# GpSimd's large-tile elementwise work moves to VectorE, and the experts' weights are split in halves of 1024 columns

## The chip, the cores and the metric

The kernel runs on one core of one Trainium2 chip. The metric is the device time of one execution in microseconds (us); the time before is the median of three runs, 1736.25 us. TensorE multiplies matrices, VectorE (DVE in the rows), ScalarE (ACT) and GpSimd (POOL) do elementwise work, each with its own queue that is worked off in order; SyncE (SP) issues the loads of the weights.

## The reference, cut to what matters

Two layers over 256 latent and 256 context tokens with 1024 features each, all in float32. Layer 0 has a gated short convolution and a dense SwiGLU network, layer 1 a differential attention and eight SwiGLU experts, of which each latent token takes two. Each norm is followed by a modulation from a conditioning vector:

```python
def modulate(xn, shift, scale):
    return xn * (1 + scale) + shift

def swiglu(a, w1, w3, w2):
    return (jax.nn.silu(a @ w1) * (a @ w3)) @ w2

for i in range(DEPTH):
    sh1, sc1, g1, sh2, sc2, g2 = adaln(c, ada_w[i], ada_b[i])
    a = modulate(rms_norm(h, norm_mix_g[i]), sh1, sc1)
    ...
    h = h + g1 * y
    a = modulate(rms_norm(h, norm_ffn_g[i]), sh2, sc2)
    ...
```

The hidden width is 2816 in every SwiGLU (22 feature tiles of 128), so the experts are eight times 11 chunks of two feature tiles.

## The kernel before

A float32 product is made of three matmuls on numbers of twelve bits: each operand is the exact sum of a high part and a low part, and `mm3` (L178 to L180) multiplies high by high, low by high and high by low. The weights come from memory in units of 1 MB, 128 partitions by 2048 columns. `Loads` issues their loads on SP in the order of use, whenever a slot for a raw unit (names `rw`, `ra`, `rp`, `rq`, `xl`, `xt`) comes free. `Parts.pump` then makes the two parts: ScalarE casts the raw unit into the high part `wh` (L79), and the low part `wl` is the raw unit minus the high part, a TENSOR_TENSOR of L83 with two inputs in SBUF. Three slots hold such pairs of parts (four in the experts), so a unit is split two or three units ahead of the matmuls that use it, as soon as TensorE is done with an older unit.

Which engine takes L83 is told by `engines(u)`, by the number u of the unit. Units 0 to 48 are layer 0, 49 to 64 the attention's first ones, from 69 on come the experts, three units to a chunk:

```python
if u >= 69:
    return [(slice(0, 1024), [(V, slice(0, 768)), (PO, slice(768, 1024))]), (slice(1024, U), [(V, slice(1024, 1664)), (PO, slice(1664, U))])]
pool = u < 12 or 12 < u < 49 and u % 2 or u == 59 or u > 60
```

Here V is VectorE and PO is GpSimd. GpSimd takes more than that: the modulation of every second or so feature tile in three operations (L322, L323, L315; VectorE needs two, L325 and L317, with ScalarE's cast L326 between), the adds of half of the context's first squares (`more`), four small products of the rotary step (L705) for each tile of queries or keys, and one scaling of heads (L697).

The stages in their order: the start (0 to 86 us in the trace), where the modulation's vectors are made by long sums over the conditioning matrices on VectorE (`ada`, L258, `junk`: one operation of 1024 columns with two SBUF inputs, accumulated into a column, four to a unit) and the first six feature tiles of the convolution's input product follow the modulated tiles as they come; the convolution (to 228 us), with eight groups of five VectorE operations `conv(j)` (L490 to L499) and 12 units of `ada` between them; the dense network (to about 635 us); the attention; the routing; and the experts (from 889 us). In a chunk of an expert, TensorE makes two tiles of the hidden layer `h` with 24 matmuls of 512 columns, transposes the gated tile `ga` (L1143), and adds 12 matmuls into `y`; the order on VectorE is `ga` (L1137), splits, `hl` (L1147, the low part of the hidden tile, which the last third of `y` waits for), splits. During chunks 2 to 9 of odd experts, and at some others, gathers for the next experts are put between (`g`, L1098 on TensorE; L1092 and L1102 on VectorE). All orders are written by hand; no scheduler changes them.

Of the kernel before, what the change touches and what calls it, by code (L numbers as in the profile page):

```python
# [37 lines left out]
class Loads:  # L38
    """Units of weights, [128, 2048] each, loaded in their order as slots come free."""
# [23 lines left out]
class Parts:  # L63
    """The units as exact sums of two parts of twelve bits, made ahead of their use."""
# [24 lines left out]
    def unit(self):  # L89
        """The next unit, for use until the next call that takes one, or until release() if it is held."""  # L90
        if not self.holding:
            self.release()
        if self.cur not in self.got:
            self.pump()
        self.spent.append(self.cur)
        self.cur += 1
        return self.got[self.cur - 1]

    def __next__(self):
        """The next block of 128 columns."""  # L100
# [8 lines left out]
    def release(self, most=99):  # L109
        """Gives back what is used up."""  # L110
# [7 lines left out]
    def give(self, n):  # L118
        """Gives back the first n of the units that are held."""
# [10 lines left out]
def backbone(ctx: ExitStack, tc: tile.TileContext, i, out, stage=9):  # L130
# [16 lines left out]
    # the weights of all products, in the order of their use  # L147
# [14 lines left out]
    def engines(u):  # L162
        """Which engine takes the second parts of which columns."""
        if u == 0:
            return [(ALL, [(V, slice(0, 1280)), (PO, slice(1280, U))])]
        if u in (3, 4, 17) or 50 <= u < 59:
            return [(ALL, [(V, slice(0, 1024)), (PO, slice(1024, U))])]
        if u >= 69:
            return [(slice(0, 1024), [(V, slice(0, 768)), (PO, slice(768, 1024))]), (slice(1024, U), [(V, slice(1024, 1664)), (PO, slice(1664, U))])]
        pool = u < 12 or 12 < u < 49 and u % 2 or u == 59 or u > 60  # L170
        return [(ALL, [(PO if pool else V, ALL)])]
# [20 lines left out]
    # ---- inputs and constants that stay  # L192
# [23 lines left out]
    def attention_constants(p):  # L216
        """Gains, rotary tables and lambda."""
# [33 lines left out]
    def ada(l, u, ns=2):  # L251
        """Two feature tiles of the modulation: units 0-7 and 12-19 hold a shift and a scale, the others gates."""
# [11 lines left out]
    def ada_pe(u):  # L264
        """The same on TensorE, from a unit with rows of the weights in the partitions, in three steps."""
# [13 lines left out]
    class Squares:  # L279
        """The sum of the squares of tiles; a sum is issued after the next tile's square."""  # L280

        def __init__(self, engine=V, pool=tp, bufs=5):
            self.acc, self.sq, self.engine, self.pool, self.bufs = None, None, engine, pool, bufs
# [7 lines left out]
        def sum(self):  # L291
            if self.sq is not None:
                if self.acc is not None:
                    self.engine.tensor_tensor(out=self.sq, in0=self.acc, in1=self.sq, op=OP.add)
                self.acc, self.sq = self.sq, None
# [12 lines left out]
    def modulate(jobs):  # L308
        """The two parts of X * rs * m[:, 1] + m[:, 0] for each (k, s, rs, m, hi, lo, pool)."""
        todo = deque()  # L310

        def low(k, s, t, m, hi, lo, pool):
            h, l = hi[:, half(s)].bitcast(F32), lo[:, half(s)]
            if pool:
                PO.tensor_tensor(out=l, in0=t, in1=h, op=OP.subtract)  # L315
            else:
                V.scalar_tensor_tensor(l, t, m[:, 0, s:s + 1], h, op0=OP.add, op1=OP.subtract)  # L317

        for k, s, rs, m, hi, lo, pool in jobs:
            t = tp.tile([P, T], F32, name=f"mt{int(pool)}", bufs=2 if pool else 3)  # L320
            if pool:
                PO.tensor_tensor(out=t, in0=X[s][k], in1=rs, op=OP.mult)  # L322
                PO.tensor_scalar(t, t, m[:, 1, s:s + 1], m[:, 0, s:s + 1], op0=OP.mult, op1=OP.add)  # L323
            else:
                V.scalar_tensor_tensor(t, X[s][k], m[:, 1, s:s + 1], rs, op0=OP.mult, op1=OP.mult)  # L325
            A.activation(hi[:, half(s)], t, AF.Identity, bias=0.0 if pool else m[:, 0, s:s + 1], scale=1.0)  # L326
            todo.append((k, s, t, m, hi, lo, pool))
# [8 lines left out]
    # ---- layer 0  # L336
# [29 lines left out]
    accs, more, rs = [Squares(V, pn, 7), Squares(V, pn, 7)], Squares(PO, pn, 7), [None, None]  # L366

    def sums(s):
        """The mean squares, tokens in the partitions."""
# [28 lines left out]
    for k in range(4):  # L398
        accs[1].put(X[1][k])
        more.put(X[1][4 + k])  # L400
    V.tensor_tensor(out=accs[1].sum(), in0=accs[1].acc, in1=more.sum(), op=OP.add)
# [30 lines left out]
    # the first six feature tiles follow the modulated tiles as they come  # L432
    def mod(k, pool):
        modulate([(k, s, rs[s], ms[k], ah[k], al[k], pool) for s in range(2)])
# [7 lines left out]
    mod(0, False)  # L442
    ms.append(next(run))
    mod(1, True)
# [6 lines left out]
    mod(2, False)  # L451
# [5 lines left out]
    mod(3, True)  # L457
    main(2)
    mod(4, True)
    ms.append(ada(0, 5))  # L460
    mod(5, False)
# [6 lines left out]
    mod(6, True)  # L468
    ms.append(ada(0, 7))
    mod(7, False)  # L470
# [8 lines left out]
    with tc.tile_pool(name="sc", bufs=1, reuse_waits="tile") as pc:  # L479
# [30 lines left out]
        # the products with the last feature tile come last  # L510
# [10 lines left out]
        def last_tiles(n, hi, lo, gates, acc, mods):  # L521
            """The last four feature tiles for the latent tokens, then for the context; each half is normalized meanwhile."""
# [6 lines left out]
            def norm(s):  # L529
                rs = rstd(mean(acc[s], st()), s)  # L530
                return [(k, s, rs, mods[k], ah[k], al[k], k % 4 == 3) for k in range(KT)]
# [819 lines left out]
```

## Time and profile before

| What | Value |
|---|---|
| runs | 1733.71, 1736.25, 1740.63 us, median 1736.25 us |
| span of the profiled execution | 1734.4 us (no other time is recorded for it) |
| TensorE busy | 1618.0 us, 93% of the span |
| VectorE busy | 1455.4 us, 84% |
| GpSimd busy | 1038.4 us, 60% |
| ScalarE busy | 885.8 us, 51% |
| from memory | 400.37 MB, 231 GB/s in the mean |

Busy shares are means over stages with different limits. A matmul of 512 columns is shown with some 0.40 us but starts 0.23 us after the one before it, so a wait of TensorE that the rows give is 0.16 us shorter than what is lost. A duration of a VectorE operation also covers a tail of some 0.06 to 0.08 us in which the next one has begun; "start to start" below is the distance of two starts.

### The profile page before, as it was taken

How to read it: one execution, taken by the hardware profiler on the slowest of the kernel's cores; microseconds unless marked ns; L12 is line 12 of the kernel's file. 1: busy time of each engine (PE TensorE's matmuls, PEld its weight loads, DVE VectorE, ACT ScalarE, POOL GpSimd, SP SyncE). 2: the span in 40 equal slices, each digit the busy share in tenths (PEclk: the TensorE clock that was granted, in tenths of full speed). 3: DMA queues.
4: the chain of work that ended last, by engine and by line, in shares of the span. 5: the costliest groups of instructions: out<-in, count | busy, mean ns of one | idle time of the engine just before them, and what ended most of it. 6: DMA issues, size and time to landing. Idle time of an engine off the chain costs nothing. (4 is left out here: it accounts for less than half of the span.)

```text
span 1734.4 us, 21267 instructions
## 1 busy us (share of the span) xinstructions
PE 1618.0 (93%) x7415; PEld 1286.6 (74%) x7415; DVE 1455.4 (84%) x1780; ACT 885.8 (51%) x1241; POOL 1038.4 (60%) x684
## 2 busy tenths in 40 slices
PE   9699889999999998996889999999999999999997
PEld 7587688788788887864667777777777876778775
DVE  6889987778558576348689999999999999999997
ACT  3222243222222244346367766777567776677774
POOL 4733224221212247413269978999788997899996
PEclk9899899999999999998989999999999999999999
DMA  8334444535446422212369988899788988789890
GB/s 341 111 132 170 170 146 132 177 136 194 170 181 260 165 98 92 80 49 102 141 224 356 350 290 312 321 358 348 294 314 319 357 330 313 300 334 356 333 350 26
DMA packets 55733, 400.37 MB, mean 231 GB/s; under 512 B 6449, under 2 KB 6481, under 8 KB 7105
## 3 DMA queue, kind: packets, MB, share of 16 engines
q1 hardware_dynamic: 55298, 398.50, 62.1%
q8 instruction: 60, 0.98, 0.2%
q0 software_dynamic: 320, 0.44, 0.2%
q14 instruction: 55, 0.45, 0.1%
HBM read 397.87 MB, written 1.05 MB: 230 GB/s over the span
## 5 line engine op out<-in xcount | busy, mean ns | idle before, releaser
L83 POOL TENSOR_TENSOR wl<-rw,wh 128x256 fp32r<-128x256 f32 (+4 forms) x190 | 401.1, 2131 | 537.8 <-ACT wh L79 419.3
L83 DVE TENSOR_TENSOR wl<-rw,wh 128x768 fp32r<-128x768 f32 (+4 forms) x178 | 264.8, 1520 | 62.3 <-ACT wh L79 60.6
L79 ACT CAST wh<-rw 128x1024 fp32r<-128x1024 f32 (+1 forms) x209 | 268.3, 1314 | 69.1 <-PE mm L179 50.5
L258 DVE SCALAR_TENSOR_TENSOR junk<-ra,cb 128x1024 bf16<-128x1024 f32 x136 | 250.9, 1845 | 3.8 <-DMA ra<-ada 0.5
L178 PE MATMUL mm<-ah,wh 128*128 128x512 f32 (+1 forms) x576 | 225.4, 391 | 16.6 <-ACT ah L326 11.9
L180 PE MATMUL mm<-ah,wl 128*128 128x512 f32 (+1 forms) x576 | 224.9, 390 | 6.7 <-POOL wl L83 6.7
L179 PE MATMUL mm<-al,wh 128*128 128x512 f32 (+1 forms) x576 | 224.8, 390 | 2.2 <-POOL al L315 2.2
L180 PE MATMUL y<-wh,hl 128*128 128x512 f32 x352 | 144.0, 409 | 20.8 <-DVE hl L1147 20.0
L83 POOL TENSOR_TENSOR wl<-ra,wh 128x384 fp32r<-128x384 f32 (+1 forms) x95 | 135.1, 1440 | 22.6 <-ACT wh L79 22.6
L178 PE MATMUL h<-wh,xl 128*128 128x512 f32 x352 | 143.2, 407 | 0.0
L178 PE MATMUL h<-wh,xs 128*128 128x512 f32 x352 | 142.8, 406 | 0.0
L83 POOL TENSOR_TENSOR wl<-rp,wh 128x256 fp32r<-128x256 f32 x96 | 137.2, 1456 | 8.3 <-ACT wh L79 7.7
L83 POOL TENSOR_TENSOR wl<-rq,wh 128x256 fp32r<-128x256 f32 x92 | 137.0, 1516 | 8.5 <-ACT wh L79 7.9
L178 PEld LDWEIGHTS mm<-ah,wh 128*128 128x128 f32 x576 | 111.4, 193 | 41.2 <-ACT ah L326 12.7
L178 PE MATMUL y<-wh,hh 128*128 128x512 f32 x352 | 141.3, 401 | 0.5 <-ACT hh L1146 0.5
L179 PE MATMUL h<-wl,xs 128*128 128x512 f32 x352 | 139.6, 397 | 0.4
L179 PE MATMUL h<-wl,xl 128*128 128x512 f32 x352 | 139.3, 396 | 0.4 <-POOL wl L83 0.3
L180 PE MATMUL h<-wh,xl 128*128 128x512 f32 x352 | 139.0, 395 | 0.0
L180 PE MATMUL h<-wh,xs 128*128 128x512 f32 x352 | 139.0, 395 | 0.0
L179 PE MATMUL y<-wl,hh 128*128 128x512 f32 x352 | 138.9, 395 | 0.0
L180 PEld LDWEIGHTS mm<-ah,wl 128*128 128x128 f32 x576 | 111.1, 193 | 31.7 <-POOL wl L83 8.2
L83 DVE TENSOR_TENSOR wl<-ra,wh 128x768 fp32r<-128x768 f32 x94 | 127.6, 1391 | 4.5 <-ACT wh L79 4.5
(291 smaller groups left out, 3696.5 us busy)
## 6 DMA issues: line engine op xcount, KB each, us to landing
rw<-moe SPq DMA_DIRECT2D x75, 1024.0 KB, 4.9
rw<-w SPq DMA_DIRECT2D x65, 1024.0 KB, 4.9
ra<-moe SPq DMA_DIRECT2D x48, 1024.0 KB, 4.9
rp<-moe SPq DMA_DIRECT2D x48, 1024.0 KB, 5.0
rq<-moe SPq DMA_DIRECT2D x46, 1024.0 KB, 4.8
ra<-ada SPq DMA_DIRECT2D x44, 1024.0 KB, 5.0
xl<-moe SPq DMA_DIRECT2D x24, 1024.0 KB, 4.9
xt<-moe SPq DMA_DIRECT2D x23, 1024.0 KB, 4.9
```

The source lines that it names most:

```text
L79: self.nc.scalar.copy(hi[:, c0], raw[:, c0])
L83: engine.tensor_tensor(out=lo[:, c], in0=raw[:, c], in1=hi[:, c].bitcast(F32), op=OP.subtract)
L178: PE.matmul(ps, wh, xh, start=first, stop=False)
L179: PE.matmul(ps, wh, xl, start=False, stop=False)
L180: PE.matmul(ps, wl, xh, start=False, stop=last)
L258: V.scalar_tensor_tensor(junk, raw[:, a * D:(a + 1) * D], 1.0, cb[:, s], op0=OP.mult, op1=OP.mult, accum_out=m[:, a, s:s + 1])
```

## The change

`engines` names VectorE alone. A unit of the experts is still split in two, now in two halves of 1024 columns with one VectorE operation each, behind ScalarE's casts of the same halves. All other units take one VectorE operation of 2048 columns. `modulate` has lost its form for GpSimd, the squares are all added on VectorE, and so are the rotary products and the scaling of heads. GpSimd keeps its DMA issues, masks, iota and the router's eight small scalings of 8 columns. The orders of ScalarE, TensorE and SP stay. Comments were dropped, so line numbers are lower behind the change (L258 becomes L253, L325 L312, L317 L308, L490 L475, L1137 L1122, L1147 L1132).

```diff
     def engines(u):
-        if u == 0:
-            return [(ALL, [(V, slice(0, 1280)), (PO, slice(1280, U))])]
-        if u in (3, 4, 17) or 50 <= u < 59:
-            return [(ALL, [(V, slice(0, 1024)), (PO, slice(1024, U))])]
         if u >= 69:
-            return [(slice(0, 1024), [(V, slice(0, 768)), (PO, slice(768, 1024))]), (slice(1024, U), [(V, slice(1024, 1664)), (PO, slice(1664, U))])]
-        pool = u < 12 or 12 < u < 49 and u % 2 or u == 59 or u > 60
-        return [(ALL, [(PO if pool else V, ALL)])]
+            return [(c, [(V, c)]) for c in (slice(0, 1024), slice(1024, U))]
+        return [(ALL, [(V, ALL)])]
...
-        for k, s, rs, m, hi, lo, pool in jobs:
-            t = tp.tile([P, T], F32, name=f"mt{int(pool)}", bufs=2 if pool else 3)
-            if pool:
-                PO.tensor_tensor(out=t, in0=X[s][k], in1=rs, op=OP.mult)
-                PO.tensor_scalar(t, t, m[:, 1, s:s + 1], m[:, 0, s:s + 1], op0=OP.mult, op1=OP.add)
-            else:
-                V.scalar_tensor_tensor(t, X[s][k], m[:, 1, s:s + 1], rs, op0=OP.mult, op1=OP.mult)
-            A.activation(hi[:, half(s)], t, AF.Identity, bias=0.0 if pool else m[:, 0, s:s + 1], scale=1.0)
+        for k, s, rs, m, hi, lo in jobs:
+            t = tp.tile([P, T], F32, name="mt", bufs=5)
+            V.scalar_tensor_tensor(t, X[s][k], m[:, 1, s:s + 1], rs, op0=OP.mult, op1=OP.mult)
+            A.activation(hi[:, half(s)], t, AF.Identity, bias=m[:, 0, s:s + 1], scale=1.0)
...
-    for k in range(4):
+    for k in range(KT):
         accs[1].put(X[1][k])
-        more.put(X[1][4 + k])
-    V.tensor_tensor(out=accs[1].sum(), in0=accs[1].acc, in1=more.sum(), op=OP.add)
...
-            PO.tensor_tensor(out=heads(x), in0=heads(x), in1=qkg[:, None, 64:].to_broadcast([P, 8, 64]), op=OP.mult)
+            V.tensor_tensor(out=heads(x), in0=heads(x), in1=qkg[:, None, 64:].to_broadcast([P, 8, 64]), op=OP.mult)
...
-                PO.tensor_tensor(out=zs[:, :, r2, b], in0=xs[:, :, r2, 1 - b],
+                V.tensor_tensor(out=zs[:, :, r2, b], in0=xs[:, :, r2, 1 - b],
```

On VectorE's queue at the start, between the vectors of feature tile 1 (`mod0_1`) and the first two sums for tile 2 (`junk`, in which `rx0` is the raw conditioning unit), there stood before:

```order
L245 TENSOR_TENSOR mod0_1_295<-st_221,adab_87 128x4
L249 TENSOR_SCALAR mod0_1_295<-mod0_1_295,gain_88 128x2
L258 SCALAR_TENSOR_TENSOR junk_309,mod0_2_308<-rx0_109,cb_83 128x1024
L258 SCALAR_TENSOR_TENSOR junk_311,mod0_2_308<-rx0_109,cb_83 128x1024
L258 SCALAR_TENSOR_TENSOR junk_313,mod0_2_308<-rx0_109,cb_83 128x1024
```

and now:

```order
L240 TENSOR_TENSOR mod0_1_294<-st_221,adab_87 128x4
L244 TENSOR_SCALAR mod0_1_294<-mod0_1_294,gain_88 128x2
L312 SCALAR_TENSOR_TENSOR mt_297<-xl_85,mod0_1_294,rs0_238 128x256
L312 SCALAR_TENSOR_TENSOR mt_300<-xc_86,mod0_1_294,rs1_244 128x256
L308 SCALAR_TENSOR_TENSOR al1_273<-mt_297,mod0_1_294,ah1_265 128x256
L308 SCALAR_TENSOR_TENSOR al1_273<-mt_300,mod0_1_294,ah1_265 128x256
L253 SCALAR_TENSOR_TENSOR junk_306,mod0_2_305<-rx0_109,cb_83 128x1024
```

The four operations of tile 1's modulation have come in ahead of the sums for tile 2; they were six on GpSimd.

In the convolution, between the second group (`yp1`, `ct`, `ul1`) and the next conditioning unit, VectorE had before:

```order
L490 TENSOR_TENSOR yp1_603<-mm_285,cs_632 128x2x256
L494 SCALAR_TENSOR_TENSOR ct_635<-yp1_603,convw_89,ct_635 128x512
L495 SCALAR_TENSOR_TENSOR ct_635<-yp1_603,convw_89,ct_635 128x512
L497 TENSOR_TENSOR ct_635<-mm_286,ct_635 128x512
L499 TENSOR_TENSOR ul1_615<-ct_635,uh1_607 128x512
L258 SCALAR_TENSOR_TENSOR junk_673,mod0_8_672<-ra0_69,cb_83 128x1024
```

and now:

```order
L475 TENSOR_TENSOR yp1_592<-mm_284,cs_621 128x2x256
L479 SCALAR_TENSOR_TENSOR ct_624<-yp1_592,convw_89,ct_624 128x512
L480 SCALAR_TENSOR_TENSOR ct_624<-yp1_592,convw_89,ct_624 128x512
L482 TENSOR_TENSOR ct_624<-mm_285,ct_624 128x512
L484 TENSOR_TENSOR ul1_604<-ct_624,uh1_596 128x512
L83 TENSOR_TENSOR wl2_79<-rw2_73,wh2_78 128x2048
L253 SCALAR_TENSOR_TENSOR junk_662,mod0_8_661<-ra0_69,cb_83 128x1024
```

One split of a whole unit (`wl2`) stands in front of the sums; it was on GpSimd, beside them.

In a chunk of the first expert, from one `hl` to the next, VectorE had before:

```order
L1147 TENSOR_TENSOR hl_6315<-ht_6311,hh_6314 128x256
L83 TENSOR_TENSOR wl0_75<-xt_4415,wh0_74 128x768
L83 TENSOR_TENSOR wl0_75<-xt_4415,wh0_74 128x640
L1137 TENSOR_TENSOR ga_6343<-h13_6297,ga_6343 128x256
L83 TENSOR_TENSOR wl1_77<-rq0_6008,wh1_76 128x768
L83 TENSOR_TENSOR wl1_77<-rq0_6008,wh1_76 128x640
L83 TENSOR_TENSOR wl2_79<-rq1_6009,wh2_78 128x768
L83 TENSOR_TENSOR wl2_79<-rq1_6009,wh2_78 128x640
L1147 TENSOR_TENSOR hl_6383<-ht_6379,hh_6382 128x256
```

and now (x2 stands for the two halves of a unit):

```order
L1132 TENSOR_TENSOR hl_6272<-ht_6268,hh_6271 128x256
L83 TENSOR_TENSOR wl0_75<-xt_4392,wh0_74 128x1024 x2
L1122 TENSOR_TENSOR ga_6298<-h13_6256,ga_6298 128x256
L83 TENSOR_TENSOR wl1_77<-rq0_5979,wh1_76 128x1024 x2
L83 TENSOR_TENSOR wl2_79<-rq1_5980,wh2_78 128x1024 x2
L1132 TENSOR_TENSOR hl_6334<-ht_6330,hh_6333 128x256
```

The places are the same; each of the six pieces has 1024 columns in place of 768 or 640, and GpSimd's six pieces of 256 or 384 columns are gone.

## Rows read from the trace of the kernel before

**Rows 1.** The page's part 1: busy time of each engine, its share, instructions.

```profile
PE 1618.0 (93%) x7415; PEld 1286.6 (74%) x7415; DVE 1455.4 (84%) x1780; ACT 885.8 (51%) x1241; POOL 1038.4 (60%) x684
```

**Rows 2.** Windows by stage: length, busy (instructions) of each engine, granted clock, DMA share, GB/s.

```profile
core 0: us, PE busy (x) PEld busy (x) DVE busy (x) ACT busy (x) POOL busy (x), PEclk, DMA share, GB/s
0.00:86.00 86.00, 68.74 (x261) 54.65 (x262) 64.38 (x95) 25.84 (x48) 51.17 (x41) 0.90 0.58 225
86.00:228.00 142.00, 127.34 (x523) 100.61 (x522) 126.87 (x157) 31.46 (x33) 39.67 (x9) 0.95 0.46 168
228.00:635.00 407.00, 403.79 (x2006) 337.62 (x2007) 290.85 (x420) 123.91 (x149) 95.78 (x39) 1.00 0.45 161
...
889.00:1734.40 845.40, 803.64 (x3588) 629.65 (x3588) 813.91 (x872) 587.41 (x766) 749.75 (x521) 1.00 0.84 312
```

**Rows 3.** Timelines of VectorE while GpSimd is idle: start, duration, engine, line, operation.

```profile
200.01 2.28 DVE L83 TENSOR_TENSOR wl<-rw,wh 128x2048 fp32r<-128x2048 f32 x1
202.22 0.68 DVE L490 TENSOR_TENSOR yp<-mm,cs 128x512 f32<-128x512 f32 x1
...
259.96 1.23 DVE L83 TENSOR_TENSOR wl<-rw,wh 128x1024 fp32r<-128x1024 f32 x1 [1.37 <-ACT wh L79]
261.11 1.75 DVE L305 RECIPROCAL rs<-rs 128x256 f32<-128x256 f32 x1
```

**Rows 4.** Timelines of VectorE and of GpSimd at the same time, in the convolution.

```profile
97.18 5.70 DVE L258 SCALAR_TENSOR_TENSOR junk<-ra,cb 128x1024 bf16<-128x1024 f32 x1
...
97.16 10.19 POOL L83 TENSOR_TENSOR wl<-rw,wh 128x2048 fp32r<-128x2048 f32 x2 [10.14 <-DVE junk L258]
```

**Rows 5.** Groups of the convolution, 86 to 228 us: count, busy, mean ns, idle before.

```profile
L258 DVE SCALAR_TENSOR_TENSOR junk<-ra,cb 128x1024 bf16<-128x1024 f32 x48 | 93.9, 1956 | 1.2
...
L83 POOL TENSOR_TENSOR wl<-rw,wh 128x2048 fp32r<-128x2048 f32 x8 | 38.6, 4842 | 87.5 <-ACT wh L79 59.4 <-DVE junk L258 28.1
```

**Rows 6.** Timelines of VectorE and of TensorE at the start.

```profile
39.53 5.52 DVE L258 SCALAR_TENSOR_TENSOR junk<-rx,cb 128x1024 bf16<-128x1024 f32 x1
...
58.46 1.19 DVE L317 SCALAR_TENSOR_TENSOR al<-mt,mod,ah 128x256 fp32r<-128x256 f32 x2 [2.51 <-ACT ah L326]
...
76.92 0.48 DVE L325 SCALAR_TENSOR_TENSOR mt<-xl,mod,rs 128x256 f32<-128x256 f32 x1
77.33 0.48 DVE L325 SCALAR_TENSOR_TENSOR mt<-xc,mod,rs 128x256 f32<-128x256 f32 x1
...
82.04 2.71 DVE L83 TENSOR_TENSOR wl<-rw,wh 128x1024 fp32r<-128x1024 f32 x1 [0.64 <-ACT wh L79]
...
52.75 0.79 PE L178 MATMUL mm<-ah,wh 128*128 128x512 f32 x1 [6.52 <-ACT ah L326]
```

**Rows 7.** Timelines of VectorE and of TensorE around one chunk of the first expert.

```profile
904.77 2.71 DVE L83 TENSOR_TENSOR wl<-rw,wh 128x768 fp32r<-128x768 f32 x2
907.40 0.41 DVE L1137 TENSOR_TENSOR ga<-h,ga 128x256 f32<-128x256 f32 x1
907.73 5.70 DVE L83 TENSOR_TENSOR wl<-rw,wh 128x768 fp32r<-128x768 f32 x4
913.36 0.41 DVE L1147 TENSOR_TENSOR hl<-ht,hh 128x256 fp32r<-128x256 f32 x1
...
904.90 0.51 PE L180 MATMUL y<-wh,hl 128*128 128x512 f32 x1 [0.97 <-DVE hl L1147]
```

**Rows 8.** Waits of TensorE's weight loads and matmuls from 889 us: total, times, longest.

```profile
PEld y L180 <- DVE hl L1147: 40.8, 49, 1.4
...
PE g L1172 <- DVE yl L1162: 6.6, 7, 1.1
```

**Rows 9.** Windows in the experts: seven chunks of an even expert; two whole experts (22 chunks).

```profile
1141.90:1202.20 60.30, 60.30 (x267) 48.47 (x266) 60.18 (x55) 46.09 (x57) 59.01 (x41) 1.00 0.95 351
1101.40:1314.30 212.90, 203.54 (x915) 159.69 (x914) 206.45 (x226) 148.60 (x198) 189.72 (x133) 1.00 0.88 326
```

**Rows 10.** Timelines of VectorE and of TensorE in the routing.

```profile
854.70 8.46 DVE L1015 TENSOR_SCALAR oh<-iota,posp 128x128 fp32r<-128x128 f32 x2
...
864.63 1.09 PE L967 MATMUL sc<-ident,xt 128*128 128x128 f32 x4 [7.05 <-DVE xt L961]
```

**Rows 11.** Timeline of VectorE between the layers.

```profile
635.25 6.79 DVE L83 TENSOR_TENSOR wl<-rw,wh 128x1024 fp32r<-128x1024 f32 x2 [1.43 <-ACT wh L79]
```

More of the change, by code (lines that the diff above doesn't have):

```diff
@@ L279, in backbone, with __init__ @@
     class Squares:
-        def __init__(self, engine=V, pool=tp, bufs=5):
-            self.acc, self.sq, self.engine, self.pool, self.bufs = None, None, engine, pool, bufs
+        def __init__(self, pool=tp, bufs=5):
+            self.acc, self.sq, self.pool, self.bufs = None, None, pool, bufs
         def put(self, x):
@@ L293, in sum @@
                 if self.acc is not None:
-                    self.engine.tensor_tensor(out=self.sq, in0=self.acc, in1=self.sq, op=OP.add)
+                    V.tensor_tensor(out=self.sq, in0=self.acc, in1=self.sq, op=OP.add)
                 self.acc, self.sq = self.sq, None
@@ L310, in modulate, with low @@
         todo = deque()
-        def low(k, s, t, m, hi, lo, pool):
-            h, l = hi[:, half(s)].bitcast(F32), lo[:, half(s)]
-            if pool:
-                PO.tensor_tensor(out=l, in0=t, in1=h, op=OP.subtract)
-            else:
-                V.scalar_tensor_tensor(l, t, m[:, 0, s:s + 1], h, op0=OP.add, op1=OP.subtract)
-        for k, s, rs, m, hi, lo, pool in jobs:
-            t = tp.tile([P, T], F32, name=f"mt{int(pool)}", bufs=2 if pool else 3)
-            if pool:
-                PO.tensor_tensor(out=t, in0=X[s][k], in1=rs, op=OP.mult)
-                PO.tensor_scalar(t, t, m[:, 1, s:s + 1], m[:, 0, s:s + 1], op0=OP.mult, op1=OP.add)
-            else:
-                V.scalar_tensor_tensor(t, X[s][k], m[:, 1, s:s + 1], rs, op0=OP.mult, op1=OP.mult)
-            A.activation(hi[:, half(s)], t, AF.Identity, bias=0.0 if pool else m[:, 0, s:s + 1], scale=1.0)
-            todo.append((k, s, t, m, hi, lo, pool))
+        def low(s, t, m, hi, lo):
+            V.scalar_tensor_tensor(lo[:, half(s)], t, m[:, 0, s:s + 1], hi[:, half(s)].bitcast(F32), op0=OP.add, op1=OP.subtract)
+        for k, s, rs, m, hi, lo in jobs:
+            t = tp.tile([P, T], F32, name="mt", bufs=5)
+            V.scalar_tensor_tensor(t, X[s][k], m[:, 1, s:s + 1], rs, op0=OP.mult, op1=OP.mult)
+            A.activation(hi[:, half(s)], t, AF.Identity, bias=m[:, 0, s:s + 1], scale=1.0)
+            todo.append((s, t, m, hi, lo))
             if len(todo) > 2:
@@ L365, in backbone @@
     A.activation(cT, cT, AF.Silu)
-    accs, more, rs = [Squares(V, pn, 7), Squares(V, pn, 7)], Squares(PO, pn, 7), [None, None]
+    accs, rs = [Squares(pn, 7), Squares(pn, 7)], [None, None]
     def sums(s):
@@ L431, in backbone, with mod @@
     first = [bank() for _ in range(6)]
-    def mod(k, pool):
-        modulate([(k, s, rs[s], ms[k], ah[k], al[k], pool) for s in range(2)])
+    def mod(k):
+        modulate([(k, s, rs[s], ms[k], ah[k], al[k]) for s in range(2)])
     def main(k, between=None):
@@ L440, in main @@
                 between()
-    mod(0, False)
+    mod(0)
     ms.append(next(run))
-    mod(1, True)
+    mod(1)
     ms.append(ada(0, 2))
@@ L450, in backbone @@
     next(run)
-    mod(2, False)
+    mod(2)
     parts.limit = 2
@@ L456, in backbone @@
     ms += [next(run), m4]
-    mod(3, True)
+    mod(3)
     main(2)
-    mod(4, True)
+    mod(4)
     ms.append(ada(0, 5))
-    mod(5, False)
+    mod(5)
     parts.limit = 3
@@ L467, in backbone @@
     ms.append(ada(0, 6))
-    mod(6, True)
+    mod(6)
     ms.append(ada(0, 7))
-    mod(7, False)
+    mod(7)
     main(4)
@@ L530, in norm @@
                 rs = rstd(mean(acc[s], st()), s)
-                return [(k, s, rs, mods[k], ah[k], al[k], k % 4 == 3) for k in range(KT)]
+                return [(k, s, rs, mods[k], ah[k], al[k]) for k in range(KT)]
             def add(f, m, s):
```

## The prediction, written before the changed kernel had run

> **What bounds the kernel now.** I read the busy times first: TensorE 93%, VectorE 84%, GpSimd 60% [rows 1]. By that page alone TensorE bounds and 116 us (1734.4 - 1618.0) at most are to be had. The windows by stage say where [rows 2]: the start (0 to 86 us) loses 17.3 us of TensorE, the convolution (86 to 228) 14.7, the dense network (228 to 635) only 3.2, the experts (889 to the end) 41.8. In the experts VectorE is busy 813.9 of 845.4 us, more than TensorE: both are nearly full, and I must see who waits for whom.
>
> Then the timelines, for what an operation of VectorE costs with GpSimd idle and with GpSimd at work. Alone, a split of 2048 columns takes 2.28 us, 2.21 from start to start, and one of 1024 takes 1.23, 1.15 from start to start [rows 3]. Beside GpSimd the sum of 1024 columns that starts at 97.18, 0.02 us after a pair of GpSimd's splits, takes 5.70 us [rows 4]. That is its own 1.2 plus 4.5 more, and GpSimd's mean for one split in this stage is 4.84 [rows 5]: VectorE stood still until GpSimd's operation was over. The Trainium skill says so too ("SBUF — State Buffer", section "Who interferes with whom": an operation of VectorE with two SBUF inputs and one of GpSimd that reads SBUF exclude each other). This rule would make every such pair take the sum of both; in the experts the trace bears it out in part only, since there pieces overlap somewhat, and I use the rows.
>
> So GpSimd's work is not free. A unit moved to VectorE adds 2.21 us there and takes away up to 4.5 of standing still. That is the whole question: is the time that VectorE gains larger than the work it takes over, and does it lie on the path?
>
> **Start, -3.** VectorE's chain of sums sets the pace; TensorE's longest wait (6.52 us before 52.75) is for a tile that GpSimd modulates [rows 6]. From 35 us on VectorE loses: two sums of the kind at 39.53, 5.52 in place of 1.23, 4.3 each; 1.5 at the split at 82.04; some 2.5 in nine sums that GpSimd's modulation stretches by 0.2 to 0.4; and waits of 2.51 and 0.64, and one of 1.3 of the same kind [rows 6]. That makes 17. It takes over two whole units (4.4) and two halves (2.1: a split of 2048 in place of one of 1024, 2.21 - 1.15 [rows 3], twice), and four tiles' modulation with four operations each, 0.41 from start to start (76.92 to 77.33) [rows 6], 6.6. That makes 13.1, and 0.2 for each of four tiles in which VectorE waits for ScalarE's cast between its two operations, 0.8. Sum: -3.2. Bounds: the new waits are a full 2.5 each (+6), or TensorE's 6.5 us go as a whole (-8).
>
> **Convolution, -15.** VectorE is busy 126.9 of 142 us [rows 2], the rest is mostly its own short waits for ScalarE in each group, so what VectorE saves, the stage saves. 48 sums take 93.9 us [rows 5]; at 1.23 they would take 59.0, so 34.9 is standing still. Eight units come from GpSimd [rows 5] at 2.21 each, 17.7. Where a split now stands in front of a group it may wait at the queue's head for ScalarE's cast, with a group's five operations behind it, which the next products wait for: I charge 1.2 in two places where VectorE would be there before the cast (an estimate from the 1.37 that a split waited for its cast [rows 3]). -34.9 + 17.7 + 2.4 = -14.8. TensorE, busy 127.3 of 142 [rows 2], allows about the same, 14.7. Bounds: waits for the cast at all eight splits give -8 (-17.2 + 8 x 1.2); none, -17.
>
> **Dense network, 0.** TensorE is busy 403.8 of 407 us here. VectorE is busy 290.9; some 16 units come to it, 35 us, which makes 326 of 407. The work that hides it is TensorE's own 404 us; if a split stood before a low part that TensorE is waiting for, it would cost up to 2.2 us a time. I take 0, from -2 to +6.
>
> **Between the layers, -3.** The two halves at 635.25 take 6.79 us [rows 11] and 2.3 alone: 4.5 lost, of which TensorE sees a part, since another product covers it. The rotary products now cost VectorE some 0.8 us a tile. I take -2.7, from 0 to -5.
>
> **Attention, 0.** Some eight splits of 2.21 [rows 3] come into VectorE's queue among the softmax's operations, and GpSimd's splits no longer stretch those that lay beside them. I read about as much stretching there as splits to come, so 0, ±3.
>
> **Routing, -3.5.** Two one-hot tiles (L1015) take 8.46 us at 854.70, though they have 128 columns each, and TensorE waits 7.05 us for what stands behind them until 864.63 [rows 10]. In their place two splits of 2.21 come ahead: the next sum starts some 3.5 us earlier. Bounds -1 and -6.
>
> **Experts, -45.** In the first expert VectorE has no gap from 904.77 to past 913.36: two pieces 2.71, `ga` 0.41, four pieces 5.70, `hl` [rows 7]. Six pieces cost 8.4 us in a chunk; `hl` comes late, and TensorE waits for it at 904.90 [rows 7]. As six halves alone they cost 6 x 1.15 = 6.9, and the chunk on VectorE 6.9 + 2 x 0.34 = 7.6. TensorE's chunk without waits is to be seen in an even expert: seven chunks in 60.30 us with TensorE busy throughout [rows 9], 8.61 each. VectorE's 7.6 is then below TensorE's 8.6, and where gathers are put in it gains TensorE's work too (VectorE some 8.4, TensorE 9.1). The bound passes from VectorE to TensorE. What does that free? TensorE is idle 41.8 us of the stage [rows 2]. A wait shows 0.16 us too short (matmuls are shown 0.39 long and start 0.23 apart), and 49 waits of the weight loads are for `hl` [rows 8]: 41.8 + 49 x 0.16 = 49.6. Of this I leave 4.6 standing: the waits for `yl` (6.6 us in 7 waits [rows 8]) hang on a chain through ScalarE and will go only in part. So -45: a pair of experts falls from 212.9 us [rows 9] to about 201.5. Bounds: -25, if a third of the waits remain because splits stand ahead of `hl`, and -51.
>
> **The sum.** -3.2 - 14.8 + 0 - 2.7 + 0 - 3.5 - 45 = -69.2. On the profiled span of 1734.4 that is 1665.2. The median of the runs, 1736.25, lies 1.9 above that span, so 1667 us. GpSimd's own 1038 us of work [rows 1] becomes next to nothing; VectorE's busy time stays near what it was.
>
> **The rivals.**
> (a) Splits that wait for ScalarE stand ahead of `hl`. The order on VectorE is the same as before, but a half of 1024 waits for ScalarE's cast of the whole half at the head of the queue. For it speaks that VectorE waits for casts already; against it that in the even expert's seven chunks, in the same order, no such wait reached TensorE [rows 9]. Then the experts give -25, other stages less by 3: 1734.4 - 46 + 1.9 = 1690.
> (b) The loads become the bound. In the seven quick chunks they ran at 351 GB/s with a share of 0.95 [rows 9]; a pair of experts moves 326 GB/s x 212.9 us = 69.4 MB [rows 9], so at 351 GB/s it takes at least 197.7 us, just under the 201.5 forecast. If only 335 can be kept up over hundreds of us, 207 us a pair, and the experts give some -24: 1690. For it: the share of 0.95; against it: 351 was kept for 60 us on end, and eleven slots for raw units smooth the rest. The Trainium skill ("SBUF — State Buffer", "A bandwidth-pool intuition that's wrong (but worth ruling out)") gives about 358 GB/s from memory to a core; by that a pair needs 193.8 us, and the loads would not bind. The trace's long stretch, at 351, agrees with it nearly.
> (c) Slower: the stretch of VectorE is not GpSimd's doing but comes from the traffic of the loads and of ScalarE. Then a piece of 1024 in the experts costs what 768 and 640 do now, 8.41 / 6 = 1.40 for 704 columns in the mean, 2.04 for 1024, and a chunk 12.9 us, against a mean of 845.4 / 88 = 9.6 [rows 2]. It decides from (9.6 - 0.7) / 6 = 1.49 us a half on. At 1.6 us a half the experts cost 88 x 0.7 = 60 us more, and elsewhere nothing is gained, since the stretches stay: 1734.4 + 60 + 1.9 = 1796. Against it: with loads going on (168 GB/s in the convolution [rows 2]) but GpSimd idle, the splits take 2.28 and 1.23 [rows 3].
> (d) Nothing is changed in the end: TensorE is 93% busy, and what VectorE gives back is lost to new waits for ScalarE's cast; within 8 us of 1736.
>
> **How the numbers follow.** My forecast (with the bounds of its terms 1652 to 1684) has a chance of 0.74; (a) 0.10, (b) 0.07, (d) 0.04, (c) 0.03, and 0.02 that more is freed than I counted. The likeliest is 1667. The range goes from 1647, where all terms take their better bound, to 1697, which holds (a) and (b). A change of 0.5%, 8.7 us, is about what a measurement can tell from none. Faster by more than that: 0.74 + 0.10 + 0.07 + 0.02 = 0.93; within it 0.04; slower 0.03.
>
> **What would show it.** In the changed profile: sums of L253 all near 1.22 us, with no long ones; halves in the experts 1.23 us; VectorE in the experts busy near 710 of 800 us, TensorE busy 98% there, waits for `hl` gone; the first group of the convolution some 3 us earlier and the dense network's start some 18 us earlier; the loads at 345 GB/s or more in the experts. I am wrong if TensorE waits for `wl` or `hl` there at all often, if SP's loads are never held back by slots (then the loads bind), or if halves are longer than 1.5 us.

## The result, and the profile after

The changed kernel takes 1668.82 us (median of 4 runs, 1667.13 to 1671.86), the kernel before 1736.99 in the same comparison. The ratio is 0.9613, 95% interval 0.9595 to 0.9631: 3.9% faster. Forecast was 1667 us, in a range from 1647 to 1697. The profiled execution has a span of 1665.3 us.

The page's part 1 of the changed kernel, the line that answers to [rows 1]:

```profile
PE 1600.8 (96%) x7415; PEld 1285.0 (77%) x7415; DVE 1328.9 (80%) x1886; ACT 885.5 (53%) x1241; POOL 13.1 (1%) x29
```

VectorE has taken over nearly all of GpSimd's work, and its own busy time fell, from 1455.4 to 1328.9 us; I had said that it would stay near what it was. The windows by stage of the changed kernel, to be held against [rows 2]; each boundary is the start of the same matmul as in the trace before:

```profile
core 0: us, PE busy (x) PEld busy (x) DVE busy (x) ACT busy (x) POOL busy (x), PEclk, DMA share, GB/s
0.00:80.67 80.67, 67.34 (x260) 52.42 (x261) 57.61 (x112) 25.75 (x48) 3.59 (x11) 0.96 0.62 236
80.67:212.83 132.16, 123.19 (x522) 97.46 (x520) 113.56 (x169) 31.56 (x34) 2.12 (x4) 1.00 0.53 185
212.83:616.87 404.04, 402.19 (x2006) 337.26 (x2007) 279.97 (x448) 125.04 (x149) 6.06 (x8) 1.00 0.46 162
616.87:668.07 51.20, 47.25 (x223) 38.05 (x222) 45.27 (x78) 24.50 (x37) 0.00 (x0) 0.97 0.35 124
668.07:816.89 148.82, 136.18 (x653) 98.95 (x652) 80.02 (x139) 73.40 (x175) 1.37 (x6) 0.94 0.28 99
816.89:861.46 44.57, 33.93 (x167) 27.15 (x165) 32.38 (x71) 20.15 (x37) 0.00 (x0) 0.81 0.38 142
861.46:1665.30 803.84, 790.74 (x3588) 633.72 (x3588) 720.10 (x872) 585.12 (x765) 0.00 (x0) 1.00 0.87 328
```

In the experts TensorE is now busier (790.7 of 803.8 us) than VectorE (720.1); before it was the other way round. Starts of the same matmuls in the two traces give what each stage became shorter by:

| Stage | forecast, us | measured, us |
|---|---|---|
| start | -3.2 | -5.2 |
| convolution | -14.8 | -9.8 |
| dense network | 0 | -3.2 |
| between the layers | -2.7 | -3.7 |
| attention | 0 | -2.4 |
| routing | -3.5 | -3.4 |
| experts | -45 | -41.4 |
| sum | -69.2 | -69.1 |

That the sum agrees to 0.1 us is luck, its terms do not: start and convolution together gave 3.0 us less than forecast, the experts 3.6 less, the dense network, the attention and the stage between them 6.6 more.

VectorE's long sums and its splits in the convolution, groups of the changed kernel, against [rows 5] (count, busy, mean ns, idle before):

```profile
L253 DVE SCALAR_TENSOR_TENSOR junk<-ra,cb 128x1024 bf16<-128x1024 f32 x48 | 58.7, 1223 | 1.2
L83 DVE TENSOR_TENSOR wl<-rw,wh 128x2048 fp32r<-128x2048 f32 x11 | 25.1, 2289 | 4.7 <-ACT wh L79 4.7
```

The same 48 sums took 93.9 us and now take 58.7, all near 1.22 us: the standing still of 35 us is gone as forecast (34.9). And one group of the experts' halves (144 of them), where [rows 7] had pairs of 2.71 us for 1408 columns:

```profile
L83 DVE TENSOR_TENSOR wl<-rw,wh 128x1024 fp32r<-128x1024 f32 x144 | 168.8, 1222 | 15.0 <-ACT wh L79 14.5 <-DMA rp<-moe 0.5
```

### The profile page after: what moved, and what is told of

Its sections match the earlier page's. It is cut to its first block, busy times and chain, and to the rows that moved or that the text cites. A ratio compares the mean times of both kernels' runs of the same rounds, so it can differ in the third digit from the quotient of the medians.

```text
span 1665.3 us, 20172 instructions
## 1 busy us (share of the span) xinstructions
PE 1600.8 (96%) x7415; PEld 1285.0 (77%) x7415; DVE 1328.9 (80%) x1886; ACT 885.5 (53%) x1241; POOL 13.1 (1%) x29
## 5 line engine op out<-in xcount | busy, mean ns | idle before, releaser
L83 DVE TENSOR_TENSOR wl<-rw,wh 128x1024 fp32r<-128x1024 f32 (+1 forms) x211 | 321.9, 1561 | 98.1 <-ACT wh L79 97.6
L253 DVE SCALAR_TENSOR_TENSOR junk<-ra,cb 128x1024 bf16<-128x1024 f32 x136 | 166.3, 1223 | 3.3
L174 PEld LDWEIGHTS mm<-al,wh 128*128 128x128 f32 x576 | 109.5, 190 | 23.8 <-DVE al L308 1.2
L83 DVE TENSOR_TENSOR wl<-ra,wh 128x1024 fp32r<-128x1024 f32 (+1 forms) x95 | 113.1, 1232 | 15.3 <-ACT wh L79 14.8
L83 DVE TENSOR_TENSOR wl<-rp,wh 128x1024 fp32r<-128x1024 f32 x96 | 112.7, 1221 | 6.4 <-ACT wh L79 6.4
L83 DVE TENSOR_TENSOR wl<-rq,wh 128x1024 fp32r<-128x1024 f32 x92 | 108.0, 1220 | 8.4 <-ACT wh L79 7.9
L79 ACT CAST wh<-rp 128x1024 fp32r<-128x1024 f32 x96 | 96.6, 1047 | 6.3 <-PE y L175 5.4
```

Of the source, the lines that this page charges most:

```text
L79: self.nc.scalar.copy(hi[:, c0], raw[:, c0])
L83: engine.tensor_tensor(out=lo[:, c], in0=raw[:, c], in1=hi[:, c].bitcast(F32), op=OP.subtract)
L174: PE.matmul(ps, wh, xl, start=False, stop=False)
L253: V.scalar_tensor_tensor(junk, raw[:, a * D:(a + 1) * D], 1.0, cb[:, s], op0=OP.mult, op1=OP.mult, accum_out=m[:, a, s:s + 1])
```

## The experiments

Ratios are to the kernel before, run on the same chip. The theory: what VectorE gains is the time that it stood still while GpSimd read SBUF, and each stage gains by itself. The rivals: GpSimd's pieces were merely late; other pieces are what helps; the stages hang on each other.

**The experts alone.** On the kernel before:

```diff
         if u >= 69:
-            return [(slice(0, 1024), [(V, slice(0, 768)), (PO, slice(768, 1024))]), (slice(1024, U), [(V, slice(1024, 1664)), (PO, slice(1664, U))])]
+            return [(c, [(V, c)]) for c in (slice(0, 1024), slice(1024, U))]
```

> The kernel before, with only the experts' units (from 69 on) split on VectorE in two halves; all else stays with GpSimd. Theory (VectorE's operations stand still while GpSimd reads; each stage gains by itself): the experts' stage, which fell from 845.4 to 803.8 us between the two traces, falls by the same 41 us here and the other stages stay, so 1737 - 41 = 1696 us. Rival (the experts only profit from what the earlier stages hand on, parts and loads that are ahead): less than half of it, above 1716 us.

1696.7 us, ratio 0.9770 (0.9753 to 0.9786). The experts lost 40.1 us between the same matmuls, all else 1.0 together. The theory holds.

**All but the experts.** The changed kernel with that line as before.

> The changed kernel, with the experts' units split as before (768 and 640 columns on VectorE, 256 and 384 on GpSimd). Theory: the experts are back at 845 us, the stages ahead of them keep their 28 us: 1737 - 28 = 1709 us. Rival (an interaction of the stages): below 1700 or above 1718 us.

1706.8 us, ratio 0.9827 (0.9810 to 0.9843): 27.6 us ahead of the experts, 2.3 in them. The parts add up: 40.8 + 30.7 = 71.5 us (1737.5 - 1696.7, 1737.5 - 1706.8) against 68.2 for both (1736.99 - 1668.82); by the spans of the profiled executions they are 41.1 and 29.9 against 69.1.

**GpSimd reads.** In `pump` of the changed kernel, ahead of VectorE's split of an expert's half:

```diff
+                if self.n >= 69:
+                    m = 2 if c0.start == 0 else 3
+                    x = self.ident[:, None, :].to_broadcast([P, m, P])
+                    o = lo[:, c0.start:c0.start + m * P].rearrange("p (m q) -> p m q", m=m)
+                    self.nc.gpsimd.tensor_tensor(out=o, in0=x, in1=x, op=OP.subtract)
...
+    parts.ident = ident
```

> The changed kernel; in the experts GpSimd subtracts a constant tile from itself, 256 and 384 columns for each unit (as many as it took before), into the columns of the low part that VectorE writes over afterwards. No result of it is used; it can start as soon as TensorE is done with the slot. Theory (contention): 640 columns cost a unit 2.71 us in place of 1.6 on VectorE before, so 1.1 us more; a unit then costs 2.3 + 1.1 = 3.4 and a chunk 3 x 3.4 + 0.7 = 10.9 us on VectorE, above TensorE's 8.6 to 9.1: the halves are shown with 1.6 us or more and the time is 1800 to 1850 us. Rival (before, GpSimd's own pieces simply came late; what GpSimd does costs VectorE nothing): 1669 to 1675 us, halves 1.22 us.

1797.1 us, ratio 1.0347 (1.0330 to 1.0364). The experts became 88.1 us longer than in the kernel before, so 129.5 longer than in the changed one. Groups of this run, VectorE's halves in the window 900 to 1600 us, then GpSimd's operations:

```profile
L88 DVE TENSOR_TENSOR wl<-rw,wh 128x1024 fp32r<-128x1024 f32 x108 | 165.8, 1578 | 8.5 <-POOL wl L86 4.7 <-issue 3.8
...
L86 POOL TENSOR_TENSOR wl<-ident 128x384 fp32r<-128x384 f32 x260 | 408.0, 1569 | 71.8 <-PE h L179 45.0 <-PE y L179 25.9
L86 POOL TENSOR_TENSOR wl<-ident 128x256 fp32r<-128x256 f32 x260 | 350.2, 1347 | 209.6 <-PE h L179 175.0 <-PE y L179 29.7 <-DVE wl L88 3.8
```

A half takes 1.58 us in the mean of this group in place of 1.22 (1.56 in the mean of all 520), though nothing that TensorE uses comes from GpSimd. VectorE waited for GpSimd's columns (POOL wl L86) for 4.7 us in this group of 108; the stretch of the group's own durations is 108 x 0.36 = 38 us. The mean hides two kinds: 147 of the 520 halves take 1.25 us in the mean, the other 373 take 1.68, and each of these 373 ends 1.08 us after the end of a GpSimd subtraction that had begun ahead of it. One such turn; VectorE's two halves, then GpSimd's subtraction:

```profile
1009.54 1.23 DVE L88 TENSOR_TENSOR wl<-rq,wh 128x1024 fp32r<-128x1024 f32 x1 [0.57 <-issue]
1010.68 1.85 DVE L88 TENSOR_TENSOR wl<-rq,wh 128x1024 fp32r<-128x1024 f32 x1
...
1009.57 1.88 POOL L86 TENSOR_TENSOR wl<-ident 128x384 fp32r<-128x384 f32 x1 [0.75 <-PE h L179]
```

The subtraction begins 0.03 us after the first half and takes 1.88 us where it takes 0.83 by itself: it stood until the half was over. The second half begins at 1010.68, stands until the subtraction ends at 1011.45, and ends 1.08 us later. So these short operations exclude each other as a whole; an operation that stands is shown as a longer one, and so the rows of the two engines overlap. The price of 3.4 us a unit that I expected was too high: two halves are 3.2 by durations.

**GpSimd writes.** At the same place, 1024 columns a half, without a read:

```diff
+                if self.n >= 69:
+                    self.nc.gpsimd.memset(lo[:, c0].bitcast(F32), 0.0)
```

> The changed kernel; in the experts GpSimd clears each half of a low part, 1024 columns, before VectorE writes it, at the same places as in the run with reads. It reads nothing. Theory (it is the reads that exclude each other): halves stay at 1.22 us and the time at 1669 us, 1680 at most for the added waits. Rival (any work of GpSimd on SBUF stretches VectorE, or the added wait alone does the harm): about as slow as the run with reads, above 1750 us.

1670.7 us, ratio 0.9614 (0.9598 to 0.9630): as the changed kernel. Groups of this run, one of the halves from 900 to 1600 us, then GpSimd's clears:

```profile
L85 DVE TENSOR_TENSOR wl<-rw,wh 128x1024 fp32r<-128x1024 f32 x126 | 147.6, 1218 | 15.0 <-issue 8.3 <-ACT wh L79 6.7
...
L83 POOL MEMSET wl<- 128x1024 f32 x520 | 492.2, 956 | 411.4 <-PE h L176 286.0 <-PE y L176 116.0 <-DVE xf L1162 6.2
```

GpSimd is busy 492 us beside the same halves at the same places, and a half stays at 1.22 us: of all 520 halves 516 overlap a clear, and none takes longer than 1.23. So it is not GpSimd's work as such, nor the added wait, but its reads. The Trainium skill ("SBUF — State Buffer", section "Who interferes with whom") states just this: an operation of VectorE with two SBUF inputs contends with GpSimd's reads of SBUF, not with an operation that only writes it. These two runs agree with it, 1.58 against 1.22 us.

**Four pieces on VectorE.** The changed kernel with 768, 256, 640 and 384 columns, all with `V`.

> The changed kernel, with the experts' units in the four pieces of before (768, 256, 640, 384 columns), all four on VectorE. Theory (the engine matters, not the pieces): each operation costs some 0.08 us beyond its columns, a unit 2.3 + 2 x 0.08, a chunk 0.5 us more on VectorE, which TensorE's 8.6 covers in even experts; in chunks 3 to 8 of odd experts, where the low part of the hidden tile is already 0.45 us late, it adds up to 0.3 us: 1669 to 1677 us. Rival (the two longer pieces are what helps): above 1690 us.

1681.7 us, ratio 0.9681 (0.9665 to 0.9697), 13 us slower than the two halves and 4.7 above the most that I expected. Between the same matmuls the experts are 12.0 us longer than in the changed kernel; the attention, which the edit leaves alone, is 3.4 longer in this profiled execution. Waits of TensorE's weight loads, of the changed kernel in its whole span:

```profile
PEld y L175 <- DVE hl L1132: 14.4, 25, 0.6
```

and with four pieces from 840 us:

```profile
PEld y L175 <- DVE hl L1132: 25.9, 25, 1.4
```

The same 25 waits, nearly twice as long. Chunks 3 to 8 of odd experts take 9.95 us in place of 9.54, even experts' chunks 8.62 in both. So the engine gives most of the gain and the pieces a part.

**Whole units.** The changed kernel without the line for the experts, so with one cast and one split of 2048 columns.

> The changed kernel, with the experts' units not halved: one cast of 2048 columns on ScalarE, then one split of 2048 on VectorE. A unit is cheaper on VectorE (2.21 in place of 2.30 us), but what stands behind it waits up to 2.2 us, and the split starts a cast of 2048 later. Theory: parts are ready two units ahead, so little shows: 1669 to 1680 us. Rival (halves are needed, because the low part of the hidden tile waits behind a whole cast and a whole split): above 1690 us.

1688.3 us, ratio 0.9722 (0.9706 to 0.9738): 19.5 us slower, 19.0 of it in the experts between the same matmuls; the theory's expectation was wrong and the halves count. The wait moves to another part; waits of the weight loads from 840 us:

```profile
PEld y L172 <- DVE wl L83: 29.6, 24, 1.7
```

24 waits, again in chunks 2 to 9 of three odd experts, which now take 10.2 us; the third unit's low part is late there.

**The gather's step ahead.** The changed kernel:

```diff
+            if n == 1 and e < NE - 1 and 2 <= c < 2 + KT:
+                got[pr + 1] = next(run)
             if last is not None:
                 e0, c0, _ = last
...
-                if 2 <= c < 2 + KT:
-                    got[pr + 1] = next(run)
```

> The changed kernel, with the gather's step in chunks 2 to 9 of odd experts issued ahead of the chunk's second product instead of behind it. In the changed kernel's trace ScalarE stands 2.8 us in such a chunk, waiting for the gathered tile that VectorE makes behind two halves; the next cast, split and hidden tile come late, and TensorE loses 0.45 us a chunk, 10.7 us in all. Theory: 1669 - 9 = 1660 us. Rival (it only moves the wait to the gathered tile or its matmuls): 1665 to 1672 us.

1668.1 us, ratio 0.9606 (0.9590 to 0.9622): no gain, as the rival had it. The first six chunks of the eight fell to 9.09 us, TensorE's own time; then VectorE, which kept its 9.54 us a chunk, used up its lead and the last two were 9.4 to 9.5 again. What the six gave was lost in the chunk ahead of the eight, which takes 12.1 us, once 13.7, in place of 10.0; there the gather's first matmul now waits for `xf`. Waits of the weight loads from 840 us:

```profile
PEld g L1083 <- DVE xf L1160: 6.0, 3, 2.0
```

**Only the units below 69.** On the kernel before:

```diff
-        if u == 0:
-            return [(ALL, [(V, slice(0, 1280)), (PO, slice(1280, U))])]
-        if u in (3, 4, 17) or 50 <= u < 59:
-            return [(ALL, [(V, slice(0, 1024)), (PO, slice(1024, U))])]
...
-        pool = u < 12 or 12 < u < 49 and u % 2 or u == 59 or u > 60
-        return [(ALL, [(PO if pool else V, ALL)])]
+        return [(ALL, [(V, ALL)])]
```

> The kernel before, with only the units below 69 split on VectorE as a whole; modulation, rotary products and the experts stay as before. Theory: the long sums of the convolution (34.9 us of standing still against 10 units of 2.21 us more) are freed by this alone: -13 there, -2 to -4 between the layers, -3 in the routing, and at the start nothing, since GpSimd's modulation stays: 1737 - 20 = 1717 us. Rival (the modulation that GpSimd keeps is what holds the start and the norms up): above 1726 us.

1706.6 us, ratio 0.9831 (0.9811 to 0.9850): 10 us more gain than expected, and the same as with all of the change but the experts (1706.8).

**ScalarE's casts of the gather one step later.** The changed kernel:

```diff
+        def high(x, k):
+            for n in range(2):
+                A.copy(xs[n][0][:, k], x[:, n])
...
-            for n in range(2):
-                A.copy(xs[n][0][:, k], x[:, n])
             if late is not None:
+                high(*late)
                 low(*late)
             late = x, k
             if k == KT - 1:
+                high(*late)
                 low(*late)
```

> The changed kernel; in the gather, ScalarE's two casts of a gathered tile are issued one step later than the tile, beside the low parts that VectorE already takes one step later. With the step moved ahead as a whole, ScalarE still stood 2.8 us in each such chunk, waiting for the gathered tile behind two halves on VectorE, and VectorE 1.1 us for the cast behind that: a loop of 9.54 us between the two engines. Theory (that loop, not TensorE, sets the pace of chunks 2 to 9 in odd experts): the wait goes, the chunks fall from 9.54 to 9.09 us, 1669 - 9 = 1660 us. Rival (VectorE's own work sets their pace): 1666 to 1670 us.

1657.2 us, ratio 0.9542 (0.9529 to 0.9555): the fastest of all, 11.6 us below the changed kernel. What was removed is seen in one chunk of the changed kernel: VectorE, then ScalarE, then TensorE:

```profile
1010.58 0.42 DVE L1132 TENSOR_TENSOR hl<-ht,hh 128x256 fp32r<-128x256 f32 x1
...
1013.52 2.35 DVE L83 TENSOR_TENSOR wl<-rw,wh 128x1024 fp32r<-128x1024 f32 x2
1015.78 0.54 DVE L1087 TENSOR_SCALAR gx<-g,mod 128x256 f32<-128x256 f32 x1
...
1017.84 2.36 DVE L83 TENSOR_TENSOR wl<-xt,wh 128x1024 fp32r<-128x1024 f32 x2 [1.11 <-ACT wh L79]
1020.12 0.42 DVE L1132 TENSOR_TENSOR hl<-ht,hh 128x256 fp32r<-128x256 f32 x1
...
1016.36 0.30 ACT L1089 CAST xl<-gx 128x128 fp32r<-128x128 f32 x1 [2.82 <-DVE gx L1087]
...
1020.59 0.50 PE L175 MATMUL y<-wh,hl 128*128 128x512 f32 x1 [0.18 <-DVE hl L1132]
```

ScalarE stands 2.82 us for `gx`, which VectorE makes behind two halves; the cast of the next unit stands behind that in ScalarE's queue, so VectorE stands 1.11 us for it, and `hl` behind that is late for TensorE. From one `hl` (1010.58) to the next (1020.12) are 9.54 us. Total waits of ScalarE for `gx` in the experts, changed kernel:

```profile
ACT xl L1089 <- DVE gx L1087: 70.8, 24, 4.0
```

and with the later casts:

```profile
ACT xl L1077 <- DVE gx L1091: 4.6, 3, 1.5
```

TensorE waits for `hl` no more; chunks 2 to 8 of odd experts take 9.09 us, as from one `ga` to the next in VectorE's timeline of this run:

```profile
1000.23 0.42 DVE L1126 TENSOR_TENSOR ga<-h,ga 128x256 f32<-128x256 f32 x1
...
1009.33 0.42 DVE L1126 TENSOR_TENSOR ga<-h,ga 128x256 f32<-128x256 f32 x1
```

The experts are 51.8 us shorter than in the kernel before.

**The splits alone.** The kernel before, with `engines` of the changed kernel; modulation, squares, rotary products and the heads' scaling stay on GpSimd.

> The kernel before with all splits on VectorE as in the changed kernel (halves in the experts, whole units elsewhere); the modulation, the squares, the rotary products and the scaling of heads stay on GpSimd. The run with the units below 69 alone gave 1706.6 us, the one with everything but the experts 1706.8. Theory (the rest of the change is worth nothing): 1706.6 - 41 = 1666 us, as the changed kernel within 4. Rival (with the splits gone from GpSimd, its other work costs or gives something): outside 1662 to 1673 us.

1667.0 us, ratio 0.9593 (0.9580 to 0.9607): the whole gain. Between the same matmuls, start and convolution lost 16.2 us together here, 15.0 in the changed kernel; the rest is equal within 0.4 us a stage.

## Why the prediction held, step by step

**What bounds the kernel** was right. GpSimd's reads made VectorE stand still, and in the experts VectorE bound TensorE. The two runs with added work on GpSimd show the cause; that its pieces were merely late is refuted. One reading of mine was wrong: that in the experts the pieces overlap somewhat. VectorE, then GpSimd, in the trace before:

```profile
909.09 1.36 DVE L83 TENSOR_TENSOR wl<-rw,wh 128x640 fp32r<-128x640 f32 x1
910.38 1.77 DVE L83 TENSOR_TENSOR wl<-rw,wh 128x768 fp32r<-128x768 f32 x1
...
909.74 1.60 POOL L83 TENSOR_TENSOR wl<-rw,wh 128x384 fp32r<-128x384 f32 x1
```

GpSimd's piece stands until VectorE's first one ends at 910.45, takes until 911.34, and VectorE's second one ends 0.81 us after that. So it is throughout: 211 of the 260 pieces of 768 columns are stretched, and each ends 0.81 to 0.82 us after a GpSimd piece; 248 of the 260 of 640 are, and each ends 0.68 to 0.69 after one. A unit costs VectorE less than the sum of all four pieces where GpSimd works beside another operation of VectorE, as beside `ga` at 907.40 [rows 7], or beside a pause of it. My sum went by the rows of whole chunks and does not hang on this.

**Start and convolution**, -18.0 forecast, -15.0 measured. By VectorE's groups, which set the pace, the start gave 1.4 us in place of 3.2 (the first group begins at 84.32 for 85.76) and the convolution 13.6 in place of 14.8. The freed time of the sums was sized right (35.2 us in the convolution); the new waits were not. VectorE stood for ScalarE's cast ahead of each of these splits; timeline of the changed kernel:

```profile
39.88 2.29 DVE L83 TENSOR_TENSOR wl<-rw,wh 128x2048 fp32r<-128x2048 f32 x1 [1.30 <-ACT wh L79]
...
60.45 2.29 DVE L83 TENSOR_TENSOR wl<-rw,wh 128x2048 fp32r<-128x2048 f32 x1 [1.31 <-ACT wh L79]
...
78.82 4.50 DVE L83 TENSOR_TENSOR wl<-rw,wh 128x2048 fp32r<-128x2048 f32 x2 [1.31 <-ACT wh L79]
```

I had charged only 0.8 us for new waits there, none for these casts, 3.9 us. Ahead of 35 us I had charged nothing for the squares' adds either: the vectors of tile 1 are made 1.2 us later than before, at 28.78 for 27.57. On the other side the short operations that make these vectors (L245, L249) had been stretched too, which I had not counted: from 35 us to the first group they took 3.6 us and now take 1.9. In the convolution 11 whole splits overlap the window where one did before; two of them are those of the row at 78.82, ahead of the first group, so eight were added, as I took from GpSimd's group. The waits for casts are 4.7 us in the window's group, 3.4 without the one at 78.82, where I had charged 2.4. That the start's tiles came sooner for TensorE (-5.2 us at the matmul, which is the boundary of the table) did not help.

**Dense network**, 0 forecast, -3.2 measured: not all waits were hidden. In the trace before TensorE waited 1.72 us before 329.36 for a hidden tile, behind a stretched sum on VectorE (5.68 at 319.62); that wait is gone, which gives 2.4 us by the starts of the matmuls. Another 1.2 are TensorE's clock: in the trace before TensorE waits 3.19 us before 227.10, the granted clock from 227.80 to 230.40 is 0.50 (1.2 GHz), and six matmuls start some 0.43 us apart; in the changed kernel's the wait is 1.30 us, the clock stays at 1.00 (2.4 GHz) and they start 0.23 apart. That is read from the traces, not tried by itself.

**Attention**, 0 forecast, -2.4 measured. TensorE's waits for the softmax's weights fell from 11.3 to 8.1 us, but whether the change did it is not shown: in the profiled executions of the eight kernels with the changed attention the stage is 2.6 us shorter to 1.0 longer than in the trace before, and with the experts alone changed, which leaves the attention as it was, it is 1.9 shorter. Between the layers it was 1.0 more than forecast.

**Routing**, -3.5 forecast, -3.4 measured, but with a wait that I had not named. Timeline of VectorE in the changed kernel, to be held against [rows 10]:

```profile
832.71 0.47 DVE L1000 TENSOR_SCALAR oh<-iota,posp 128x128 fp32r<-128x128 f32 x2
...
842.33 2.29 DVE L83 TENSOR_TENSOR wl<-rw,wh 128x2048 fp32r<-128x2048 f32 x1 [3.06 <-ACT wh L79]
844.53 0.22 DVE L982 SCALAR_TENSOR_TENSOR lg<-o,ms,shl 128x8 f32<-128x8 f32 x1
```

The pair of one-hot tiles takes 0.47 us in place of 8.46. But at 842.33 a split stands 3.06 us for its cast, and the router's logits behind it; TensorE waits 4.2 us for them. This is rival (a) in one place outside the experts.

**Experts**, -45 forecast, -41.4 measured. The mechanism was right: the bound passed to TensorE, and its chunks in even experts take the 8.6 us that [rows 9] showed, but for those with gathers. A pair of experts in the middle takes 201.8 us where I had said about 201.5; the last pair, whose second expert gathers nothing, gained less. The share that stays was put in the wrong place. I left 4.6 us for `yl`, and of those waits one of 0.4 is left; I left nothing for `hl` in odd experts, and there 24 waits of some 0.45 us, 11 us, stayed, the loop of VectorE and ScalarE that the later casts removed. The sizes of the work were right, some 8.4 us on VectorE and 9.1 on TensorE in such a chunk; the step that failed was to take the longer of the two for the chunk's time, where VectorE also stands 1.11 us for a cast that waits for VectorE itself. With the loop gone, the stage gained 51.8 us, close to the -51 that I gave as the better bound.

**The rivals.** (a) held in part, in the odd experts and in the routing. (b) did not bind: a pair of experts in the middle moved 345 GB/s and seven chunks of an even expert 357, with TensorE busy throughout in these, where (b) needed 335 to be the most; and SP's loads were held back by slots that VectorE had yet to free, in 249 waits of the stage. Neither 351 nor 358 GB/s is a ceiling in this kernel: the changed kernel's page has a slice of 41.6 us at 374. Windows of the changed kernel, a pair and the seven chunks:

```profile
1061.65:1263.45 201.80, 200.51 (x913) 160.57 (x912) 183.68 (x226) 148.27 (x198) 0.00 (x0) 1.00 0.92 345
1099.28:1159.62 60.34, 60.34 (x268) 48.49 (x267) 53.47 (x57) 45.99 (x57) 0.00 (x0) 1.00 0.96 357
```

(c) is refuted by the halves of 1.22 us, (d) by the time. The range's lower end, 1647, was said to take all better bounds; by my own bounds they add up to 1644. The bounds of the forecast, 1652 to 1684, follow from no sum of my terms' bounds.

**The signs.** Sums and halves of 1.22 us, VectorE's 720.1 us and TensorE's 98% in the experts, 345 GB/s in a pair and loads that slots hold back came as I had said. The first group of the convolution came 1.4 us earlier in place of 3, the dense network 15.0 in place of 18, and the waits for `hl` did not go: by my own sign, that TensorE must not wait for `hl` often, I was wrong in the odd experts.

**The expectations** that failed were those on the changed kernel's odd experts: four pieces cost 12 us in the experts and whole units 19, since in that loop an extra tenth on VectorE is paid nearly in full (0.41 us a chunk of the some 0.5 that I had reckoned for four pieces); and moving the gather's step did not break the loop, as ScalarE's wait for `gx` went along with it (56.8 us of it stayed). The unit-below-69 run showed a wrong sizing too: I gave 8 us to the moved modulation and rotary products, and they are worth nothing measurable.

## What to carry to other kernels

A second engine for elementwise work is no help where its reads make the first one stand still: look for operations whose duration has two values, one of them with the other engine's operation beside it, and compare the sum before splitting work between the two. Here GpSimd took 4.6 us for a split that VectorE does in 2.2, and the sum of VectorE beside it stood for all of that [rows 4]. Once an engine is freed, look for loops between in-order queues: an operation that waits at a queue's head delays everything behind it, so issue it a step later, behind work that is ready. One edit of several may carry the whole gain; here it was the table of the splits.

## What the runs showed of the hardware that was not expected

GpSimd may be busy 492 us with clears of 1024 columns (0.96 us each) beside VectorE's two-input operations without either being stretched (1.22 us a half), while subtractions of 256 and 384 columns stretch them to 1.56 in the mean. I had expected some harm from the clears.

VectorE's splits and GpSimd's subtractions excluded each other as a whole in the experts too, short as they are: all 373 stretched halves end 1.08 us after a subtraction of GpSimd, and GpSimd's, which take 0.61 us (256 columns) and 0.82 (384) at the least, stand in their turn and are shown with 1.35 and 1.57 us in the mean.

An operation need not have two input tiles to be stretched: in the trace before, the one-hot TENSOR_SCALARs of [rows 10], with one tile of 128 columns and a scalar, take 4.01 and 4.53 us beside GpSimd's splits, and 0.47 for both in the changed kernel. A RECIPROCAL of one tile was not stretched: 1.74 us at 641.96, all of it beside a split of GpSimd, and 1.75 with GpSimd idle [rows 3].
